# Running the 64-row matmuls of a four-sublayer streaming-encoder trunk over 128 rows, with zeros in the unwanted rows

## The chip, the cores and the metric

One core of one Trainium2 chip runs the whole program; the other cores are idle. The metric is the time of one execution on the device in microseconds (us), median over the runs shown. Engines by the names of the profile: PE is TensorE's matmul, PEld its weight load, DVE is VectorE, ACT is ScalarE, POOL is GpSimd, SP is SyncE, which here only issues DMAs.

## The reference, cut to what matters

The input is 256 positions of 2048 features. Layer 0 mixes by a chunked gMLP and a Mamba-2 scan side by side, layer 1 by multi-head latent attention; each is followed by a gated MLP with a causal convolution, and a final RMS norm ends it. Everything is fp32. The two places that the change touches are these lines of the reference:

```python
# Mamba-2: decay between positions, from the cumulated a = dt * A of each of 32 heads
a_cum = jnp.cumsum(da, -1)
decay = jnp.exp(segsum(da))                 # exp(a_cum[i] - a_cum[j]), lower triangle
y_diag = jnp.einsum("bcgls,bcgels,bcsgep->bclgep", cb, decay, xd)
...
# attention: 16 heads; the scores are a sum of a 128-wide part and a rotary part of 64
sc = (jnp.einsum("bqhd,bkhd->bhqk", q_nope[:, q0:kend], k_nope[:, :kend])
      + jnp.einsum("bqhr,bkr->bhqk", q_pe[:, q0:kend], k_pe[:, :kend]))
```

The rotary key `k_pe` is one for all heads; the rotary query is one of 64 rows for each head.

## The kernel before, in words

**Weights.** All weights stream once from memory in units of 128 x 1024 fp32 (`load`, L167), and each unit is turned into a pair of float32r parts, `hi` by an ACT copy (L198) and `lo` by a DVE subtraction (L199). `AHEAD, LOADS = 2, 3` (L162) says how many units ahead of the matmuls a unit is converted and loaded. Activations are kept as the same kind of pair side by side in one 128 x 512 tile.

**Matmul loops.** `wstat` (L237) holds a 128 x 128 weight tile still and streams the activations: one matmul of 512 columns with `hi`, one of 256 with `lo`, for each weight tile. `astat` (L250) holds the activations and streams the weights: three matmuls of 416 or 512 columns for each half of the positions. Both write the PSUM tiles `acc`. Between them, `tick()` runs one step of a background generator from the list `bg`, so that smaller work is woven into the long matmul loops at places fixed in the code; a scheduler then sets each engine's order from the program's dependences.

**Layer 0, the scan.** `dt_prep` (L498) leaves the cumulated decays of 32 heads in `cst` (L469), a tile of 64 partitions: rows 0 to 31 hold the float32r high part of each head's sums over 256 positions, rows 32 to 63 the low part (L533, L534). `selr` is a constant that picks rows h and h + 32. `ssd(g)` (L612), a background generator run once for each of four groups of eight heads, does four steps of two heads. Each step broadcasts the two heads' sums to all 128 partitions by two matmuls over 64 rows (L627), lets DVE (L634), ACT (L636) and DVE (L641) make the decay matrices from them, and multiplies these with the inputs by matmuls of 64 columns, 128 rows deep (L652). There are 32 broadcasts in all.

**Layer 1, attention.** `latent_out` (L841) makes the rotary key: its 64 columns of weights are given twice, so that rows 0 to 63 and 64 to 127 of `kr` are equal. `roped` (L830) rotates them and writes `krope` (L814), 128 rows by 256 positions. The loop at L933 handles two heads per turn: six `wstat` calls of four weight tiles each make the rotary queries of both heads (64 rows each in one 128-row tile `qr`), two queries and two keys. The scores of the heads before (`scores`, L876), the transposes of their probabilities (`turn`, L896) and the products with the values (`values`, L902) stand between these calls. For each head and each half of the queries, `scores` issues a matmul over 128 rows and then one over 64 rows into the same columns of PSUM, all four in plain fp32, which the profile records as two matmuls each:

```python
r0 = (hh % 2) * 64
for t, (o, n) in enumerate(HALF):           # n = 128, then 256 columns
    mm(ps[:, o:o + n], qn[:, t * P:(t + 1) * P], kk[:, :n], start=True, stop=False)
    mm(ps[:, o:o + n], qr[r0:r0 + 64, t * P:(t + 1) * P], krope[r0:r0 + 64, :n], start=False, stop=True)
```

**Buffers.** 2 KB tiles come from `slot()` (61 buffers), 1 KB tiles from `tmp()` (10 buffers), PSUM from two pools of four banks, `acc` and `ms`.

Of the kernel before, what the change touches and what calls it, by code (L numbers as in the profile page):

```python
# [17 lines left out]
P = 128  # L18
# [16 lines left out]

# [1 line left out]
def stat_stream(w, cols=None, front=0):  # L37
    """[K, N] -> units [U, 128, 1024]: eight 128x128 tiles each, k fastest;
    of the first `front` column tiles the last two k tiles come after the rest."""
    if cols is not None:  # L40
        w = w[:, cols]
    k, n = w.shape
    t = w.reshape(k // P, P, n // P, P).transpose(2, 0, 1, 3)
    if front:
        a = t[:front]
        t = np.concatenate([a[:, :-2].reshape(-1, P, P), a[:, -2:].reshape(-1, P, P), t[front:].reshape(-1, P, P)])
    t = t.reshape(-1, 8, P, P)
    return np.ascontiguousarray(t.transpose(0, 2, 1, 3)).reshape(-1, P, 1024)


def mov_stream(w, cw):
    """[K, N] -> units [U, 128, 2*cw]: two k tiles of a chunk of cw columns each."""
    k, n = w.shape
    t = w.reshape(k // 256, 2, P, n // cw, cw).transpose(3, 0, 2, 1, 4)
    return np.ascontiguousarray(t).reshape(-1, P, 2 * cw)
# [43 lines left out]

# [1 line left out]
@with_exitstack  # L101
def trunk(ctx: ExitStack, tc: tile.TileContext, a, out):
# [40 lines left out]

# [1 line left out]
    seq = []  # L145
# [21 lines left out]
    def load():  # L167
        """one DMA of weights; the first ones bring the input along."""
        i = st["load"]
        if i >= len(seq):  # L170
            return
        st["load"] += 1
        ap, u, wd = seq[i]
        raw = wp.tile([P, 1024], F32, tag="raw", name=nm("raw"), bufs=4)[:, :wd]
        nc.sync.dma_start(out=raw, in_=ap[u])
        raws.append(raw)
        if i == 0:
            nc.sync.dma_start(out=vec[:, :KD], in_=a["vec"][:, :KD])
        if i < KD // 2:
            nc.sync.dma_start(out=h2[i], in_=a["x0"][i])  # L180
        if i == KD // 2:
            nc.sync.dma_start(out=con, in_=a["con"])
            nc.sync.dma_start(out=vec[:, KD:], in_=a["vec"][:, KD:])

    def convert():
        """weights as a pair of float32r parts whose sum is exact."""
        i = st["conv"]
        if i >= len(seq):
            return
        st["conv"] += 1  # L190
        raw, wd = raws[i], seq[i][2]
        raws[i] = None
        hi = wp.tile([P, 1024], F32R, tag="hi", name=nm("hi"))
        lo = wp.tile([P, 1024], F32R, tag="lo", name=nm("lo"))
        n = 2 if i < 2 else 1
        for c in range(n):
            q = slice(c * wd // n, (c + 1) * wd // n)
            A.copy(out=hi[:, q], in_=raw[:, q])  # L198
            V.tensor_tensor(lo[:, q], raw[:, q], hi[:, q].bitcast(F32), op=ALU.subtract)  # L199
        ready.append((hi, lo))  # L200
# [20 lines left out]

# [1 line left out]
    bg = []  # L223
# [47 lines left out]
    def split(src, scale=None, dst=None):  # L271
        """[128,256] fp32 (SBUF or PSUM), times a per-partition scale -> [hi | lo]."""
        x = slot(F32R) if dst is None else dst
        if scale is None:
            A.copy(out=x[:, :S], in_=src)
            V.tensor_tensor(x[:, S:], src, x[:, :S].bitcast(F32), op=ALU.subtract)  # L276
        else:
            A.activation(x[:, :S], src, AF.Identity, bias=0.0, scale=scale)  # L278
            V.scalar_tensor_tensor(x[:, S:], src, scale, x[:, :S].bitcast(F32), op0=ALU.mult, op1=ALU.subtract)  # L279
        return x  # L280

    def newton(y, v, t):
        """y = v ** -0.5"""
        V.tensor_scalar(y.bitcast(I32), v.bitcast(I32), -0.5, 1597463007.0, op0=ALU.mult, op1=ALU.add)
        for _ in range(3):
            V.tensor_tensor(t, y, y, op=ALU.mult)
            V.scalar_tensor_tensor(t, t, -0.5, v, op0=ALU.mult, op1=ALU.mult)
            V.scalar_tensor_tensor(y, t, 1.5, y, op0=ALU.add, op1=ALU.mult)
# [6 lines left out]

# [1 line left out]
    warm = cp.tile([P, 512], mybir.dt.bfloat16, name="warm")  # L297
# [5 lines left out]

# [1 line left out]
    con = cp.tile([P, CONST.shape[1]], F32, name="con")  # L305
# [13 lines left out]

# [1 line left out]
    class Sq:  # L321
        """sum of squares over feature tiles; the last tile goes its own way."""

# [45 lines left out]
        def spread(self, n):  # L369
            """the factor for feature-major tiles alone, on every partition."""  # L370
            ps = pmis()
# [8 lines left out]
    def pending(sq, n=D, wait=6, hold=None):  # L380
        """the RMS factor, made a few steps into the next matmuls."""
        box = {}

        def gen():
            for _ in range(wait):
                yield
            box["v"] = sq.finish(n, hold) if hold else sq.spread(n)
            yield

        bg.append(gen())  # L390
        return box

# [1 line left out]
    class Lazy(list):  # L394
        """entries are made when the matmul loop first reaches them."""

# [16 lines left out]

    # small tables that the layers read later
    row = cp.tile([P, 96], F32, name="row")
# [5 lines left out]
    def small_loads():  # L421
        pin(nc.gpsimd.dma_start(out=row, in_=a["row"].partition_broadcast(P)))
        yield
        for i in range(2):
            # spatial weights [j, g, i], block-lower-triangular part
            pin(nc.gpsimd.dma_start(out=wsT[i], in_=a["wsT"][:, i * 512:(i + 1) * 512]))
# [10 lines left out]

# [1 line left out]
    cosT = cp.tile([P, S], F32, name="cosT")  # L439
# [23 lines left out]

    # ================= layer 0 mixer =================
    dtt = cp.tile([P, 2, 32], F32, name="dtt")
    cum = cp.tile([P, 2, 32], F32, name="cum")
    w0 = cp.tile([P, 32], F32, name="w0")
    e1 = cp.tile([P, 32], F32, name="e1")
    cst = cp.tile([64, S], F32R, name="cst")  # L469

    def gate_z(pst, c):
        """silu of a chunk of z; for chunk 0 the first 32 columns are dt."""
        o = []
# [24 lines left out]
    def dt_prep():  # L498
# [15 lines left out]
        for t in range(2):  # L514
            for r in range(2):
                V.scalar_tensor_tensor(dad[:, t, r, :], dtt[:, t, :], -1.0, ea, op0=ALU.mult, op1=ALU.mult)
        pin(V.tensor_copy(out=selr, in_=C("sel")))
        for _ in range(20):
            yield
# [11 lines left out]
        for t in range(2):  # L531
            mm(ps[:64, t * P:(t + 1) * P], dad[:, t].rearrange("p a b -> p (a b)"), C("tri"), start=True, stop=True)
        A.copy(out=cst, in_=ps[:64, :S])  # L533
        V.tensor_tensor(cst[32:64, :], ps[32:64, :S], cst[32:64, :].bitcast(F32), op=ALU.subtract)  # L534
# [5 lines left out]
    def conv_tile(b, wname, n, width, taps, bias):  # L540
        """causal depthwise conv of a [128,256] tile along the free axis."""
        o = tmp()
# [69 lines left out]
    def ssd(g):  # L612
# [10 lines left out]
        for hp in range(4):  # L623
            ps = pmis()
            for i in range(2):
                hh = h0 + 2 * hp + i
                mm(ps[:, i * S:(i + 1) * S], selr[:64, hh:hh + 1].to_broadcast([64, P]), cst, start=True, stop=True)  # L627
            yield
# [34 lines left out]

    # gMLP, four chunks of 512 channels, the scan's groups woven in
    ya, late = [], []
# [48 lines left out]

    # gating by z, grouped RMS norm, back to feature-major
    yb = [None] * 16
# [35 lines left out]
    def residual(kt, xin, wname, last=False, front=0):  # L752
        """front: that many tiles run ahead through all but the last two k tiles."""
        sq = Sq()
# [54 lines left out]

    # ================= layer 1 mixer (MLA) =================  # L810
    box = pending(sq)
    ckv, cq, sk, sqq = [], [], Sq(), Sq()
    kr = slot()[:, :S]
    krope = slot()[:, :S]  # L814

# [14 lines left out]
    def roped(x, o):  # L830
        """rotate the halves of two 64-row heads."""
        G.tensor_tensor(o, x, cosT, op=ALU.mult)
# [8 lines left out]
    def latent_out(i, ps):  # L841
        if i == 4:
            scaled(ps, kr)
            roped(kr, krope)
            return
# [30 lines left out]
    def scores(hh, qr, qn, kk):  # L876
        ps = pmis()
        r0 = (hh % 2) * 64
        for t, (o, n) in enumerate(HALF):
            mm(ps[:, o:o + n], qn[:, t * P:(t + 1) * P], kk[:, :n], start=True, stop=False)  # L880
            mm(ps[:, o:o + n], qr[r0:r0 + 64, t * P:(t + 1) * P], krope[r0:r0 + 64, :n], start=False, stop=True)
        sc = slot()
# [29 lines left out]
    def step(kind, j):  # L912
        """one stage of the attention of heads 2j and 2j + 1."""
        if not 0 <= j < 8:
# [53 lines left out]

# [1 line left out]
    _, R, Rp = sq.finish(D)  # L970
# [84 lines left out]
```

## Time and profile before

| what | value |
|---|---|
| median of 3 runs | 2423.49 us |
| the three runs | 2418.5, 2423.49, 2424.66 us |
| the profiled execution: span from first to last instruction (its time is not listed apart from the runs) | 2419.3 us |
| PE busy | 2386.0 us, 99% of the span, 13479 matmul records |
| PEld busy | 2072.6 us, 86% |
| DVE, ACT, POOL busy | 1582.7 us (65%), 1189.3 us (49%), 482.7 us (20%) |
| mean granted TensorE clock | 0.995 of full speed |
| DMA | 0.6 of the engines' time, 180 GB/s |

Matmuls are pipelined: a record of one matmul overlaps the next one's, so a busy share of 99% does not by itself say that the array is fed without pause. The spacing of the starts says that, and the timeline gives the starts. The timeline merges instructions of the same line, operation and tiles into one row, and shows the form (rows * columns of the weights, then the streamed shape) of the first of them.

### The profile page before, as it was taken

How to read it: one execution, taken by the hardware profiler on the slowest of the kernel's cores; microseconds unless marked ns; L12 is line 12 of the kernel's file. 1: busy time of each engine (PE TensorE's matmuls, PEld its weight loads, DVE VectorE, ACT ScalarE, POOL GpSimd, SP SyncE). 2: the span in 40 equal slices, each digit the busy share in tenths (PEclk: the TensorE clock that was granted, in tenths of full speed). 3: DMA queues.
4: the chain of work that ended last, by engine and by line, in shares of the span. 5: the costliest groups of instructions: out<-in, count | busy, mean ns of one | idle time of the engine just before them, and what ended most of it. 6: DMA issues, size and time to landing. Idle time of an engine off the chain costs nothing.

```text
span 2419.3 us, 35301 instructions
## 1 busy us (share of the span) xinstructions
PE 2386.0 (99%) x13479; PEld 2072.6 (86%) x13479; DVE 1582.7 (65%) x2371; ACT 1189.3 (49%) x1729; POOL 482.7 (20%) x452
## 2 busy tenths in 40 slices
PE   8999999999999999999999999999999999999997
PEld 6888888988888888888888887788888888888886
DVE  7677777665576666666555577778666666664544
ACT  5654444644455555555444445544555555554442
POOL 4111221022211112111111132123211111111111
PEclk9999999999999999999999999999999999999998
DMA  6565545666666666666666655356666666666664
GB/s 219 166 178 156 160 153 153 188 184 189 184 190 188 189 191 191 191 189 189 191 190 191 190 170 155 96 158 185 196 188 189 190 191 191 188 190 190 191 191 131
DMA packets 121913, 435.54 MB, mean 180 GB/s; under 512 B 13696, under 2 KB 14080, under 8 KB 121744
## 3 DMA queue, kind: packets, MB, share of 16 engines
q1 hardware_dynamic: 120672, 431.02, 59.3%
q8 instruction: 105, 1.72, 0.3%
q0 software_dynamic: 352, 1.10, 0.2%
q10 hardware_dynamic: 720, 1.18, 0.1%
q14 instruction: 64, 0.52, 0.1%
HBM read 431.15 MB, written 2.10 MB: 179 GB/s over the span
## 4 chain that ended last, share of the span: by engine, by line
PE 95%; DVE 2%; issue 1%; POOL 1%; ACT 1%; DMA 0%; SPq 0%; DVEq 0%; POOLq 0%; ACTq 0%
PE acc L133 91%; PE ms L133 4%; DVE lo L199 1%; PE ms L136 1%; DVE s L279 0%; ACT hi L198 0%; DMA raw<-in_z 0%; POOL t L550 0%; DVE t L545 0%; DVE s L979 0%; POOL s L818 0%; DVE s L276 0%; POOL t L331 0%; DVE s L634 0%; DVE t L268 0%
## 5 line engine op out<-in xcount | busy, mean ns | idle before, releaser
L133 PE MATMUL acc<-s,hi 128*128 128x512 f32 x5936 | 2072.9, 394 | 0.0
L133 PE MATMUL acc<-s,lo 128*128 128x256 f32 x5936 | 1656.4, 279 | 3.8 <-DVE lo L199 3.8
L199 DVE TENSOR_TENSOR lo<-raw,hi 128x1024 fp32r<-128x1024 f32 (+2 forms) x824 | 1015.9, 1233 | 700.1 <-ACT hi L198 693.9
L198 ACT CAST hi<-raw 128x1024 fp32r<-128x1024 f32 (+2 forms) x824 | 858.0, 1042 | 1088.3 <-PE acc L133 883.4
L133 PEld LDWEIGHTS acc<-s,hi 128*128 128x128 f32 x5936 | 1112.4, 187 | 255.6 <-issue 3.2
L133 PEld LDWEIGHTS acc<-s,lo 128*128 128x128 f32 x5936 | 1118.8, 188 | 5.6 <-DVE lo L199 4.8
L133 PE MATMUL acc<-hi,s 128*128 128x512 f32 (+1 forms) x640 | 198.6, 385 | 6.2 <-DVE s L279 5.7
L331 POOL TENSOR_TENSOR t<-h 128x256 f32<-128x256 f32 x60 | 66.9, 1114 | 588.1 <-DVE h L771 563.9
L801 POOL TENSOR_TENSOR t<-t,R 128x256 f32<-128x256 f32 x88 | 121.4, 1380 | 313.8 <-ACT t L800 309.9
L798 POOL TENSOR_TENSOR t<-t,R 128x256 f32<-128x256 f32 x88 | 68.9, 783 | 488.7 <-DVE t L268 453.4
L133 PEld LDWEIGHTS acc<-hi,s 128*128 128x128 f32 x640 | 121.4, 192 | 23.7 <-DVE s L279 8.4
L545 DVE SCALAR_TENSOR_TENSOR t<-t,vec,t 128x255 f32<-128x255 f32 (+2 forms) x248 | 120.7, 487 | 14.2 <-ACT t L543 9.7
L133 PE MATMUL acc<-lo,s 128*128 128x416 f32 (+1 forms) x320 | 121.8, 381 | 1.4 <-DVE lo L199 1.4
L268 DVE TENSOR_TENSOR t<-acc,t 128x256 f32<-128x256 f32 x233 | 97.4, 418 | 0.8 <-ACT t L267 0.8
L267 ACT COPY t<-acc 128x256 f32<-128x256 f32 x233 | 83.5, 359 | 0.3 <-PE acc L133 0.3
L133 PE MATMUL ms<-s,s 128*128 128x128 f32 (+4 forms) x424 | 78.2, 307 | 1.1 <-DVE s L930 0.6
L133 PEld LDWEIGHTS ms<-s,s 128*128 128x128 f32 (+1 forms) x424 | 60.1, 189 | 19.9 <-issue 9.0
L342 POOL TENSOR_TENSOR sqacc<-sqacc,t 128x256 f32<-128x256 f32 x60 | 72.8, 1213 | 4.7
L543 ACT ACTIVATE t<-t,vec 128x256 f32<-128x256 f32 x112 | 67.2, 600 | 12.9 <-POOL t L798 7.6
L133 PEld LDWEIGHTS acc<-lo,s 128*128 128x128 f32 x320 | 61.5, 192 | 8.4 <-DVE lo L199 2.1
L279 DVE SCALAR_TENSOR_TENSOR s<-h,vec,s 128x256 fp32r<-128x256 f32 x64 | 56.6, 895 | 1.0 <-ACT s L278 1.0
L803 DVE TENSOR_TENSOR t<-t,t 128x256 f32<-128x256 f32 x88 | 37.4, 426 | 28.6 <-POOL t L801 28.6
(174 smaller groups left out, 811.7 us busy)
## 6 DMA issues: line engine op xcount, KB each, us to landing
raw<-in_up SPq DMA_DIRECT2D x352, 512.0 KB, 4.2
raw<-in_down SPq DMA_DIRECT2D x176, 512.0 KB, 3.6
raw<-in_wout SPq DMA_DIRECT2D x64, 512.0 KB, 3.6
raw<-in_z SPq DMA_DIRECT2D x40, 416.0 KB, 3.6
raw<-in_x SPq DMA_DIRECT2D x32, 512.0 KB, 3.6
raw<-in_v SPq DMA_DIRECT2D x32, 512.0 KB, 3.7
raw<-in_u SPq DMA_DIRECT2D x32, 512.0 KB, 3.9
raw<-in_wo SPq DMA_DIRECT2D x32, 512.0 KB, 3.6
```

The costliest lines, as they stand in the source:

```text
L133: return nc.tensor.matmul(*args, **kw)
L198: A.copy(out=hi[:, q], in_=raw[:, q])
L199: V.tensor_tensor(lo[:, q], raw[:, q], hi[:, q].bitcast(F32), op=ALU.subtract)
L267: A.copy(out=b, in_=ps[:, S:])
L268: V.tensor_tensor(b, ps[:, :S], b, op=ALU.add)
L279: V.scalar_tensor_tensor(x[:, S:], src, scale, x[:, :S].bitcast(F32), op0=ALU.mult, op1=ALU.subtract)
L331: eng.tensor_tensor(q, src, src, op=ALU.mult)
L342: eng.tensor_tensor(self.acc, self.acc, q, op=ALU.add)
L543: A.activation(o, b, AF.Identity, bias=bias, scale=taps[width - 1])
L545: V.scalar_tensor_tensor(o[:, i:], b[:, :S - i], taps[width - 1 - i], o[:, i:], op0=ALU.mult, op1=ALU.add)
L798: G.tensor_tensor(b, b, R, op=ALU.mult)
L801: G.tensor_tensor(o, o, R, op=ALU.mult)
```

## The change

The matmuls over 64 rows become matmuls over 128 rows. In the scan, `cst` has 128 partitions; rows 64 to 127 are set to zero once by a DVE multiplication of a constant with 0, and the broadcast uses all 128 rows of `selr` and `cst`. In attention, `krope` becomes 512 wide: columns 0 to 255 hold the rotated key in rows 0 to 63 and zeros below, columns 256 to 511 hold zeros and the key in rows 64 to 127. Two POOL memsets write the zeros; `roped` writes a 1 KB tile `ro`, and two ACT copies of 64 rows move it into place. `scores` streams 128 rows of `krope`, from the half that belongs to the head, against all 128 rows of `qr`. (The change also drops comments and docstrings.)

```diff
-    cst = cp.tile([64, S], F32R, name="cst")
+    cst = cp.tile([P, S], F32R, name="cst")
...
         pin(V.tensor_copy(out=selr, in_=C("sel")))
+
+        pin(V.tensor_scalar(cst[64:], con[64:, :S], 0.0, None, op0=ALU.mult))
...
-        A.copy(out=cst, in_=ps[:64, :S])
+        A.copy(out=cst[:64], in_=ps[:64, :S])
...
-                mm(ps[:, i * S:(i + 1) * S], selr[:64, hh:hh + 1].to_broadcast([64, P]), cst, start=True, stop=True)
+                mm(ps[:, i * S:(i + 1) * S], selr[:, hh:hh + 1].to_broadcast([P, P]), cst, start=True, stop=True)
...
-    krope = slot()[:, :S]
+
+    krope = slot()
+    G.memset(krope[64:, :S], 0.0)
+    G.memset(krope[:64, S:], 0.0)
...
             scaled(ps, kr)
-            roped(kr, krope)
+            ro = tmp()
+            roped(kr, ro)
+            for e in range(2):
+                A.copy(out=krope[e * 64:(e + 1) * 64, e * S:(e + 1) * S], in_=ro[e * 64:(e + 1) * 64])
             return
...
-        r0 = (hh % 2) * 64
+        r0 = (hh % 2) * S
         for t, (o, n) in enumerate(HALF):
             mm(ps[:, o:o + n], qn[:, t * P:(t + 1) * P], kk[:, :n], start=True, stop=False)
-            mm(ps[:, o:o + n], qr[r0:r0 + 64, t * P:(t + 1) * P], krope[r0:r0 + 64, :n], start=False, stop=True)
+            mm(ps[:, o:o + n], qr[:, t * P:(t + 1) * P], krope[:, r0:r0 + n], start=False, stop=True)
```

The order of PE is the same in both kernels, matmul for matmul. On PE, in the scan of the second group, the order after the change reads as follows (`ms` <- `s`,`s` are the products of 64 columns, `cst`,`selr` the broadcasts, `acc` the long loop):

```order
L133 MATMUL ms_2412<-s_1449,s_2395 128x64
L133 MATMUL ms_2426<-cst,selr 128x256
L133 MATMUL ms_2411<-s_1434,s_2395 128x64
L133 MATMUL ms_2426<-cst,selr 128x256
L133 MATMUL ms_2412<-s_1449,s_2395 128x64
L133 MATMUL ms_2461<-cst,selr 128x256 x2
L133 MATMUL acc_2373<-hi_2419,s_231 128x512
```

Nothing moved there: each group has two broadcasts that stand alone between products and three pairs.

On ACT, where the latents of layer 1 are made, the order before (`hi` is a converted weight unit, `s`<-`s`,`vec` the normed key latents):

```order
L278 ACTIVATE s_13422<-s_13265,vec 128x256
L267 COPY t_13460<-acc_13326 128x256
L198 CAST hi_13493<-raw_13469 128x1024
L278 ACTIVATE s_13430<-s_13318,vec 128x256
L267 COPY t_13514<-acc_13402 128x256
L198 CAST hi_13524<-raw_13491 128x1024
```

and after the change:

```order
L278 ACTIVATE s_13428<-s_13268,vec 128x256
L267 COPY t_13466<-acc_13329 128x256
L198 CAST hi_13499<-raw_13475 128x1024
L852 COPY s_13052<-t_13398 64x256 x2
L278 ACTIVATE s_13436<-s_13321,vec 128x256
L267 COPY t_13520<-acc_13408 128x256
L198 CAST hi_13530<-raw_13497 128x1024
```

The two copies into `krope` stand between a weight conversion and the last normed latent.

On POOL, at the start of the same stage, the order after the change:

```order
L342 TENSOR_TENSOR sqacc_11102<-sqacc_11102,t_12921 128x256
L818 MEMSET s_13052 64x256
L819 MEMSET s_13052 64x256
L823 TENSOR_TENSOR s_13161<-t_13162,R_13098 128x256
```

The two memsets stand between the last sum of squares of the layer before and the first scaled latent. Beside these, DVE has the one multiplication into `cst` (after the cast of `selr`, L517), and ACT's copy into `cst` (L533) now stands one place earlier, ahead of a silu.

## Rows read from the trace of the kernel before

**Rows 1.** The page: the span, PE's busy time, and the chain of work that ended last by engine and line.

```profile
span 2419.3 us, 35301 instructions
PE 2386.0 (99%) x13479; PEld 2072.6 (86%) x13479; DVE 1582.7 (65%) x2371; ACT 1189.3 (49%) x1729; POOL 482.7 (20%) x452
...
PE 95%; DVE 2%; issue 1%; POOL 1%; ACT 1%; DMA 0%; SPq 0%; DVEq 0%; POOLq 0%; ACTq 0%
```

**Rows 2.** Groups of instructions by line and shape, whole span: the matmuls over 64 rows on PE, weight loads over 128 and 64 rows on PEld (columns: rows * columns of the weights, streamed shape, count | busy us, mean ns | idle before, us), and ACT's weight conversion with what it waited for.

```profile
L133 PE MATMUL ms<-s,s 64*128 64x256 f32 x32 | 11.1, 428 | 0.0
L133 PE MATMUL ms<-cst,selr 64*128 64x256 f32 x32 | 9.0, 341 | 0.0
L133 PE MATMUL ms<-s,s 64*128 64x128 f32 x32 | 7.8, 322 | 0.0
...
L133 PEld LDWEIGHTS ms<-s,s 128*128 128x128 f32 x360 | 50.7, 190 | 12.7 <-issue 3.7 <-DVE s L930 0.9 <-DVE s L641 0.7
L133 PEld LDWEIGHTS ms<-s,s 64*128 64x128 f32 x64 | 9.4, 184 | 7.2 <-issue 5.3
...
L198 ACT CAST hi<-raw 128x1024 fp32r<-128x1024 f32 x782 | 822.4, 1052 | 1054.9 <-PE acc L133 859.8 <-issue 191.3 <-DVE lnt L286 1.8
```

**Rows 3.** Timeline of PE in the scan (columns: start us, us, engine, line, operation, tiles, form of the first, count).

```profile
297.35 0.60 PE L133 MATMUL ms<-s,s 128*128 128x128 f32 x4
...
298.02 0.39 PE L133 MATMUL acc<-lo,s 128*128 128x512 f32 x1
298.24 0.40 PE L133 MATMUL acc<-hi,s 128*128 128x512 f32 x1
298.57 0.50 PE L133 MATMUL ms<-cst,selr 64*128 64x256 f32 x2
...
299.34 0.40 PE L133 MATMUL acc<-lo,s 128*128 128x512 f32 x1
```

**Rows 4.** Timeline of PE at a sum of squares: two records of 256 columns in fp32 over 128 rows, in the long loop.

```profile
1675.57 0.59 PE L133 MATMUL ms<-sqacc,con 128*128 128x256 f32 x2
...
1676.24 0.28 PE L133 MATMUL acc<-s,lo 128*128 128x256 f32 x1
1676.36 0.39 PE L133 MATMUL acc<-s,hi 128*128 128x512 f32 x1
```

**Rows 5.** Timeline of PE at the scores of two heads, from their first matmul to the second matmul of the loop that follows.

```profile
1509.68 4.14 PE L133 MATMUL ms<-s,s 128*128 128x128 f32 x16
1513.75 0.50 PE L133 MATMUL acc<-s,hi 128*128 128x512 f32 x1
1514.09 0.28 PE L133 MATMUL acc<-s,lo 128*128 128x256 f32 x1
```

**Rows 6.** Timeline of PEld, the weight loads, at the first head of the same scores, up to the second head's first load (in brackets: idle time before, and what ended it).

```profile
1509.57 1.14 PEld L133 LDWEIGHTS ms<-s,s 128*128 128x128 f32 x6
1511.04 0.29 PEld L133 LDWEIGHTS ms<-s,s 64*128 64x128 f32 x2 [0.33 <-issue]
1511.66 1.13 PEld L133 LDWEIGHTS ms<-s,s 128*128 128x128 f32 x6 [0.33 <-issue]
```

**Rows 7.** Timeline of PE in the scan's second group: the broadcasts that stand alone, and (from 262.46) products of 64 columns with no broadcast between.

```profile
254.39 0.67 PE L133 MATMUL ms<-s,s 128*128 128x64 f32 x4
254.99 0.38 PE L133 MATMUL ms<-cst,selr 64*128 64x256 f32 x1
...
255.66 0.38 PE L133 MATMUL ms<-cst,selr 64*128 64x256 f32 x1
...
256.34 0.50 PE L133 MATMUL ms<-cst,selr 64*128 64x256 f32 x2
...
262.46 0.55 PE L133 MATMUL ms<-s,s 128*128 128x64 f32 x4
...
263.13 0.55 PE L133 MATMUL ms<-s,s 128*128 128x64 f32 x4
```

**Rows 8.** Timelines of ACT and DVE ahead of the product at 254.39, and of DVE at the first softmax.

```profile
250.47 1.06 ACT L198 CAST hi<-raw 128x1024 fp32r<-128x1024 f32 x1 [1.36 <-PE acc L133]
253.91 1.12 DVE L641 SCALAR_TENSOR_TENSOR s<-s,dtt,s 128x128 f32<-128x128 f32 x4
1488.68 0.56 DVE L883 TENSOR_TENSOR s<-ms,con 128x384 f32<-128x384 f32 x1 [1.53 <-PE ms L133]
```

**Rows 9.** Busy time of each engine in one turn of the attention loop (columns: window, length, busy us and count of PE, PEld, DVE, ACT, POOL, granted clock, DMA share, GB/s).

```profile
1513.20:1526.40 13.20, 13.20 (x75) 10.48 (x75) 10.72 (x29) 6.76 (x19) 3.43 (x6) 1.00 0.37 115
```

**Rows 10.** The rows nearest to the added instructions, by line and shape (a POOL memset, a DVE multiplication with a constant, ACT's copy into `cst`), and ACT's and POOL's timelines where the latents are made.

```profile
L427 POOL MEMSET s<- 64x256 f32 x2 | 0.8, 382 | 10.9 <-DMA s<-in_wsT 10.9
L452 DVE TENSOR_SCALAR t<-t 128x256 f32<-128x256 f32 x1 | 0.3, 293 | 0.0
L533 ACT CAST cst<-ms 64x256 fp32r<-64x256 f32 x1 | 0.4, 366 | 0.5 <-PE ms L133 0.5
1444.07 0.51 ACT L278 ACTIVATE s<-s,vec 128x256 fp32r<-128x256 f32 x1 [1.00 <-DVE s L826]
1410.10 1.70 POOL L818 TENSOR_TENSOR s<-t,R 128x256 f32<-128x256 f32 x1 [23.71 <-DVE R L288]
```

**Rows 11.** Busy time and granted clock in two stretches of the scan's third group (columns as in rows 9).

```profile
307.00:310.40 3.40, 3.19 (x17) 2.22 (x15) 3.40 (x9) 1.18 (x2) 0.00 (x0) 1.00 0.51 159
310.50:314.00 3.50, 3.50 (x9) 2.77 (x9) 1.47 (x6) 0.10 (x1) 0.00 (x0) 0.51 0.61 164
```

## The prediction

> **What bounds the kernel now.** I read the page first. PE is busy for 2386.0 of 2419.3 us and carries 95% of the chain that ended last [rows 1], so a PE microsecond saved is a microsecond of the result wherever no other engine is close behind. The second view says whether one is: ACT's weight conversion sat idle for 1054.9 us in all, 859.8 of them until PE was through with a buffer [rows 2]. The converters wait for PE, not PE for them. What is left to ask is what the array does inside its 99%, and that needs the timelines, where the distance from one start to the next is the price of a matmul.
>
> The prices over 128 rows come from undisturbed places. Four fp32 records of 128 columns and one float32r matmul of 512 take 298.02 − 297.35 = 0.67 us, and the 512 columns alone 298.24 − 298.02 = 0.22 [rows 3]; with 0.23 for it, a record of 128 columns is 0.11. Two records of 256 columns and the 512 take 1676.24 − 1675.57 = 0.67, so such a record is 0.22; the float32r matmul of 256 columns is 1676.36 − 1676.24 = 0.12 [rows 4].
>
> Now the same sums where rows change. The scores of two heads are 16 fp32 records, eight of 128 and eight of 256 columns, alternating between 128 and 64 rows. With one 512 behind them they should take 8 x 0.11 + 8 x 0.22 + 0.23 = 2.87 us. They take 1514.09 − 1509.68 = 4.41 [rows 5]. The weight loads show where it goes: at the changes between 128 and 64 rows that come behind 256 columns, the load begins late, after 0.33 us of idle time that ends by "issue", no other engine [rows 6] (behind 128 columns the gap is too short to split the row). The reader should see that the next load doesn't run under the matmul before, as it does elsewhere. And the first matmul after the last change takes 1514.09 − 1513.75 = 0.34 instead of 0.23 [rows 5].
>
> **What the change removes.** Scores: 4.41 − 2.87 = 1.54 us for two heads, eight times: **12.3 us**. Broadcasts: a pair between two matmuls of 512 columns takes 299.34 − 298.24 = 1.10 us, against 2 x 0.23 + 2 x 0.12 = 0.70 [rows 3, 4]: 0.40. Three pairs in each of four groups make 12 x 0.40 = 4.8 us. The two that stand alone: eight records of 64 columns and two broadcasts take 256.34 − 254.39 = 1.95 us. Four such records and a 512 take 263.13 − 262.46 = 0.67, so 0.11 each, and the whole should take 8 x 0.11 + 2 x 0.12 = 1.12 [rows 4, 7]. Of the 0.83 between them some 0.09 is the way into the pair that follows, counted with the pair; 0.74 x 4 = 3.0 us, of which I take 2.8, since the first of those records were also waiting on DVE's last product there [rows 8]. Broadcasts in all: **7.6 us**. Sum: 19.9 us. The rows changed are 64 + 32 records [rows 2]; each 64-row run of a score has two changes, 64 in all, and five runs of broadcasts in each of four groups have 40, so 104 changes at 0.19 us.
>
> Does a change cost nothing once both sides have 128 rows? The matmul streams the same columns and gets as many weight columns, and the 128-row records around it show no gap when `ms` follows `acc` or fp32 follows float32r [rows 3, 4]. The bounds of what goes: from nothing to all 19.9. I take all, since the rows over 128 rows are the very same instructions but for the rows.
>
> [...]
>
> **What it adds.** One DVE multiplication of 64 x 256, by the nearest row 0.29 us [rows 10], behind the sums that PE waits for in that place, once: nothing, and 0.3 us if it were all on the path. Two POOL memsets of 0.38 us each, at a place where POOL then sits idle for 23.71 us [rows 10]: nothing as long as their buffer is free, and with all of it on the path 0.8. Two ACT copies of 64 x 256, 0.37 us each by the copy into `cst`; they stand ahead of a latent for which ACT idles for 1.00 us [rows 10], so 0.74 fits, and 0.7 is the bound from above. ACT's copy into `cst`, one place earlier, adds nothing: it is the same work. No DMA is added or moved.
>
> **What could be late next.** A faster PE arrives earlier at work that DVE and ACT prepare. In the scan, the first product at 254.39 [rows 7] follows closely on DVE's four matrices, begun at 253.91 and all done at 255.03; the chain in front of them begins with a weight conversion that waited 1.36 us for PE to free its buffer [rows 8]. So it starts earlier when PE is earlier, and the small slack stays what it is. At the first softmax DVE waited 1.53 us for PE's scores [rows 8], so that chain moves along too. In a turn of the attention loop DVE is busy for 10.72 us of 13.20 [rows 9]; the turn shrinks to 13.20 − 1.54 = 11.7, still above 10.72. I put 0 to 2 us on all of this and take 0.4.
>
> **The sum.** 19.9 − 0.4 = 19.5 us off the profiled execution's span of 2419.3. That span lies 4.2 us under the median of the runs shown, 2423.5, and close to their fastest; I set the difference against the median: 2423.5 − 19.5 = **2404.0 us**.
>
> **The rivals.**
>
> *Waits take the gain back (0.08).* If DVE is the true pace of the scan, the products wait for what the broadcasts saved and all 7.6 us there are lost; and if DVE's turn, 10.72 us with no idle time allowed, stretches by one late conversion of some 1.2 us, the eight turns lose most of (11.7 − 10.72), say 0.6 each, 4.8 us. For it: DVE is the second busiest engine, with the slacks above. Against: the converters' waits on PE [rows 2, 8]. Time: 2423.5 − 19.9 + 7.6 + 4.8 = 2416.
>
> *Rows don't matter (0.05).* The pause might belong to the fp32 rotary operands or to the accumulation into the same columns, not to the 64 rows; then it stays, and the time stays at 2423.5. Against: fp32 over 128 rows runs without it [rows 4], and the broadcasts, which are float32r and don't accumulate, have it too [rows 3]. [...] The loads themselves agree (184 ns over 64 rows, 190 over 128 [rows 2]); it is the wait in front of them that is lost.
>
> *The clock falls (0.03), slower.* [...]
>
> **How the numbers follow.** The forecast has 0.84. Its own range: from 2404.0 down by 1.7 for the clock and 3 for the scatter of the runs, up by 3.4 (all added work and waits at their bounds, 3.8, less the 0.4 taken) and 3: 2399 to 2410. To leave out no more than 2 in 10, I keep that and widen it by one to two microseconds, for prices that I read from one place each: 2398 to 2412. A change within 0.3% (7.3 us), about what a measurement here can tell from none, lies between 2416.2 and 2430.8. The first rival's 2416 is at that border; half of it counts as faster. Faster: 0.84 + 0.04 = 0.88. Same: 0.05 + 0.04 = 0.09. Slower: 0.03.
>
> **What would show it.** On the timeline of PE, the scores of two heads with the 512 behind should take 2.9 us, not 4.41, in all eight turns, and a pair of broadcasts with its neighbours 0.70, not 1.10. The weight loads of these should show no idle time by "issue". If these spacings shrink and the end doesn't move, new idle time must stand on PE, ended by DVE's matrices of the scan or its softmax, and the first rival is right. If the spacings stay with all rows at 128, my reading of the pause is wrong. A granted clock below 0.99 in many of the scan's stretches would speak for the third.

## The result and the profile after

The changed kernel takes 2402.03 us, median of 4 runs (2400.11 to 2403.32); the kernel before takes 2421.69, median of 4 (2418.5 to 2424.66). The ratio is 0.9925 with an interval of 0.9912 to 0.9938, so it is faster by 18.2 us (15.0 to 21.3); the medians differ by 19.7. The forecast was 2404.0 with a range of 2398 to 2412. The profiled execution is the one of 2403.32 us, with a span of 2401.5.

The page of the changed kernel, the same lines as [rows 1]: the span, the busy times, and the chain that ended last.

```profile
span 2401.5 us, 35306 instructions
PE 2368.9 (99%) x13479; PEld 2078.8 (87%) x13479; DVE 1584.1 (66%) x2372; ACT 1189.9 (50%) x1731; POOL 482.5 (20%) x454
...
PE 95%; DVE 3%; issue 1%; ACT 1%; POOL 1%; DMA 0%; SPq 0%; DVEq 0%; POOLq 0%; ACTq 0%
```

PE has the same 13479 records and 17.1 us less busy time; the span fell by 17.8. The chain is still PE's. DVE's share of it reads 3% instead of 2%; the view rounds to whole per cent, so that step says little by itself. Where DVE came in is shown below.

The matmuls that were widened, grouped by line and shape as in [rows 2] (columns: rows * columns of the weights, streamed shape, count | busy us, mean ns | idle before).

```profile
L133 PE MATMUL ms<-s,s 128*128 128x64 f32 x128 | 19.1, 259 | 1.6 <-DVE s L643 1.6
L133 PE MATMUL ms<-s,s 128*128 128x256 f32 x64 | 16.5, 380 | 0.0
...
L133 PE MATMUL ms<-cst,selr 128*128 128x256 f32 x32 | 7.9, 313 | 0.0
```

No group with 64 rows is left. The 256-column records of the scores took 11.2 us for 32 and 11.1 for another 32 before; all 64 now take 16.5. The first row shows something new: 1.6 us of idle time in front of the scan's products, ended by DVE's decay matrices.

The timeline of PE at the scores of two heads, the same matmuls as in [rows 5].

```profile
1501.54 2.86 PE L133 MATMUL ms<-s,s 128*128 128x128 f32 x16
1504.05 0.58 PE L133 MATMUL acc<-s,hi 128*128 128x512 f32 x1
1504.47 0.28 PE L133 MATMUL acc<-s,lo 128*128 128x256 f32 x1
```

1504.47 − 1501.54 = 2.93 us, against 4.41 before and 2.87 forecast. Of the eight turns six take 2.85; this one and the first, with 2.96, are the longest. The weight loads of the same stretch, as in [rows 6]:

```profile
1501.51 2.49 PEld L133 LDWEIGHTS ms<-s,s 128*128 128x128 f32 x16
```

One unbroken row where there were three with gaps of 0.33 us. A pair of broadcasts between long matmuls, as in [rows 3], here in the scan's second group:

```profile
244.93 0.40 PE L133 MATMUL acc<-hi,s 128*128 128x512 f32 x1
245.16 0.40 PE L133 MATMUL ms<-cst,selr 128*128 128x256 f32 x2
...
245.65 0.39 PE L133 MATMUL acc<-lo,s 128*128 128x512 f32 x1
```

From the start ahead of the pair to the second one behind it: 245.65 − 244.93 = 0.72, against 1.10 before and 0.70 forecast.

Where did the 17.8 us of the span come from? PE's order is the same in both kernels, so the starts of the same matmul can be subtracted, place by place. The scores in the eight turns of attention are shorter by 1.48 to 1.57 us each, 12.4 us together. The first group of the scan is shorter by 1.29, the second by 1.31, the fourth by 1.36, and the third by 2.95, of which some 1.6 is a clock fall that is gone. That makes 19.3. Two new clock falls take 1.6 and 1.45 of it back, and 1.14 of the second is regained where PE waited before (further down). The remaining 0.4 us is spread.

### The profile page after: what moved, and what is told of

Read it like the earlier page. It is cut to its first block, busy times and chain, and to the rows that moved or that the text cites. A ratio compares the mean times of both kernels' runs of the same rounds, so it can differ in the third digit from the quotient of the medians.

```text
span 2401.5 us, 35306 instructions
## 1 busy us (share of the span) xinstructions
PE 2368.9 (99%) x13479; PEld 2078.8 (87%) x13479; DVE 1584.1 (66%) x2372; ACT 1189.9 (50%) x1731; POOL 482.5 (20%) x454
## 4 chain that ended last, share of the span: by engine, by line
PE 95%; DVE 3%; issue 1%; ACT 1%; POOL 1%; DMA 0%; SPq 0%; DVEq 0%; POOLq 0%; ACTq 0%
PE acc L133 91%; PE ms L133 3%; DVE lo L199 1%; PE ms L136 1%; ACT hi L198 0%; DVE s L279 0%; POOL t L552 0%; DMA raw<-in_z 0%; DVE t L547 0%; DVE s L987 0%; DVE s L276 0%; POOL t L683 0%; DVE s L636 0%; DVE t L268 0%; POOL t L841 0%
## 5 line engine op out<-in xcount | busy, mean ns | idle before, releaser
L198 ACT CAST hi<-raw 128x1024 fp32r<-128x1024 f32 (+2 forms) x824 | 858.4, 1042 | 1079.2 <-PE acc L133 875.6
L268 DVE TENSOR_TENSOR t<-acc,t 128x256 f32<-128x256 f32 x233 | 97.0, 416 | 0.8 <-ACT t L267 0.8
L133 PE MATMUL ms<-s,s 128*128 128x128 f32 (+3 forms) x424 | 66.6, 292 | 2.2 <-DVE s L643 1.6
L133 PEld LDWEIGHTS ms<-s,s 128*128 128x128 f32 x424 | 59.9, 190 | 9.7 <-issue 3.5
```

The source lines that it names most:

```text
L133: return nc.tensor.matmul(*args, **kw)
L268: V.tensor_tensor(b, ps[:, :S], b, op=ALU.add)
```

## The experiments

The kernel before ran beside each of them. Its median was 2420.17 (19 runs) beside the two with one part alone, the reordered scores and the two halves of the rows, 2420.38 (17 runs) beside the dummies and the added work, and 2420.19 (9 runs) beside the two with a multiplication moved to DVE.

**Each part alone.** The theory was that the change is a sum of two savings on PE with one price per change of rows, so that attention alone gives the 12.3 us that the prediction's sum has for it. The first kernel is the changed one with the scan put back:

```diff
-    cst = cp.tile([P, S], F32R, name="cst")
+    cst = cp.tile([64, S], F32R, name="cst")
...
-        pin(V.tensor_scalar(cst[64:], con[64:, :S], 0.0, None, op0=ALU.mult))
...
-                mm(ps[...], selr[:, hh:hh + 1].to_broadcast([P, P]), cst, start=True, stop=True)
+                mm(ps[...], selr[:64, hh:hh + 1].to_broadcast([64, P]), cst, start=True, stop=True)
```

> The attention half of the change alone: scores over 128 rows, the scan's broadcasts still over 64. [...] Rival (waits on DVE take the gain back in attention): under 8 us off, and new idle time on PE by the softmax.

Measured: 2406.94 us, ratio 0.9944 (0.9932 to 0.9957), 13.2 us faster. In its trace the scores of two heads take 2.85 us in six of eight turns, and 2.92 in the turn shown above.

The second is the changed kernel with attention put back:

```diff
-    krope = slot()
-    G.memset(krope[64:, :S], 0.0)
-    G.memset(krope[:64, S:], 0.0)
+    krope = slot()[:, :S]
...
-            mm(..., qr[:, t * P:(t + 1) * P], krope[:, r0:r0 + n], start=False, stop=True)
+            mm(..., qr[r0:r0 + 64, t * P:(t + 1) * P], krope[r0:r0 + 64, :n], start=False, stop=True)
```

> The scan's half of the change alone: broadcasts over 128 rows, scores as before. Theory with the full price: 40 changes go, 7.6 us off. What the trace after shows instead: 1.3 to 1.4 us off in each of the later three groups, so 5.4 us off, because the first product of a group then waits for DVE for about 0.5 us where it waited for 0.2 or less. Rival (rows don't matter): 0.

Measured: 2414.25 us, ratio 0.9977 (0.9967 to 0.9986), 5.9 us faster. The two parts add up to 19.1 us, the whole of the change (18.2 by the ratio, 19.7 by the medians). Attention gave what the sum had for it, the scan less, though the interval (3.4 to 8.0 us) alone does not exclude the 7.6 of the forecast; the matched starts of the changed kernel, 1.3 us for a group instead of 1.9, do.

**Is it the change of rows, or the 64-row matmul itself?** Both would have given the same forecast. The third kernel is the one before, with all its matmuls over 64 rows, in another order: the scores of a head run over 128, 64, 64, 128 rows. That leaves 32 of the 64 changes in the scores.

```diff
         for t, (o, n) in enumerate(HALF):
-            mm(..., qn[...], kk[...], start=True, stop=False)
-            mm(..., qr[r0:r0 + 64, ...], krope[r0:r0 + 64, ...], start=False, stop=True)
+            for r in ((0, 1) if t == 0 else (1, 0)):   # r = 1: the rotary part
+                mm(..., start=(r == t), stop=(r != t))
```

> The kernel before, with 64-row matmuls everywhere, but the scores of a head issued as 128, 64, 64, 128 rows instead of 128, 64, 128, 64: two changes a head instead of four, the same matmuls. Theory (a price for each change): 32 changes go, 32 x 0.195 = 6.2 us off. Rival (a price for each 64-row matmul, or for the fp32 rotary operands): 0.

Measured: 2415.22 us, ratio 0.9976 (0.9967 to 0.9985), 5.0 us faster. The timeline of PE at the scores of two heads in this kernel:

```profile
1507.04 3.56 PE L133 MATMUL ms<-s,s 128*128 128x128 f32 x16
...
1510.67 0.28 PE L133 MATMUL acc<-s,lo 128*128 128x256 f32 x1
```

3.63 us, as in all eight turns but the first, half way between 4.41 and the 2.85 of most turns after the change: half of the changes, half of the price, with every 64-row matmul still there. So the price belongs to the change. 0.78 x 8 = 6.2 us for 32 changes is 0.195 each.

**The price of one change by itself.** Three kernels each add 88 small float32r matmuls of 128 columns to the changed kernel, one at a time inside the long loops of the gated MLPs, between matmuls over 128 rows (their results are used nowhere):

```diff
             psg = wstat(KD, xs)
+            mm(dps[:, :P], cst[:64, :P], cst[:64, P:], start=True, stop=True)   # 64 rows
+            mm(dps[:, :P], cst[:, :P], cst[:, P:], start=True, stop=True)       # or: 128 rows
+            mm(dps[:64, :P], cst[:, :64], cst[:, P:], start=True, stop=True)    # or: 64 columns
             psv = wstat(KD, xs)
```

> The changed kernel with one more matmul, of no use to the result, in each of the 88 steps of the two gated MLPs, between two long loops: float32r, 128 columns, over 64 rows. Theory: each costs its own 0.05 to 0.11 us and two changes of rows, 2 x 0.19 us: 38 to 43 us more than the changed kernel. Rival (a price for each 64-row matmul, not for the change back): half of that.

> The same 88 added matmuls over 128 rows. Theory: 0.05 to 0.11 us each, 5 to 10 us more than the changed kernel, so 33 us less than with 64 rows.

> The same 88 added matmuls over 128 rows but with 64 columns of weights, so that they write 64 partitions. If a change in the columns of the array costs what a change in its rows does: 38 to 43 us more than the changed kernel. If it costs nothing: 5 to 10.

Measured, one execution each: spans of 2468.2, 2432.0 and 2438.1 us. What costs is the difference between the kernels: (2468.2 − 2432.0) / 88 = 0.41 us for a lone matmul over 64 rows, 0.206 for each of its two changes. By matched starts 36.1 of these 36.2 us stand in the loops with the dummies. PE's timeline at one dummy over 64 rows:

```profile
721.82 0.28 PE L133 MATMUL acc<-s,lo 128*128 128x256 f32 x1
722.03 0.32 PE L133 MATMUL ms<-cst 64*128 64x128 f32 x1
722.29 0.50 PE L133 MATMUL acc<-s,hi 128*128 128x512 f32 x1
722.62 0.28 PE L133 MATMUL acc<-s,lo 128*128 128x256 f32 x1
```

and over 128 rows:

```profile
720.69 0.28 PE L133 MATMUL acc<-s,lo 128*128 128x256 f32 x1
720.80 0.22 PE L133 MATMUL ms<-cst 128*128 128x128 f32 x1
720.86 0.45 PE L133 MATMUL acc<-s,hi 128*128 128x512 f32 x1
721.15 0.28 PE L133 MATMUL acc<-s,lo 128*128 128x256 f32 x1
```

From the first start to the last, 0.80 against 0.46 us. The start before the dummy is 0.21 away instead of 0.11, the dummy itself holds the array for 0.26 instead of 0.06, and the one behind it for 0.33 instead of 0.29. The loss stands in front of both changes and a little behind. It is 0.34 us at the dummy, 0.17 for a change, on the average of all 88 too; the other 0.07 is spread over the matmuls between the dummies, and what causes it was not found. The waits of the weight loads (PEld, us in total, times, longest) show it in the kernel with 64 rows,

```profile
PEld ms L133 <- issue: 26.9, 97, 1.0
```

and in the one with 128 rows:

```profile
PEld ms L133 <- issue: 4.7, 9, 1.0
```

88 more waits, 22 us more: idle time of the weight load "by issue" is the sign by which such a change is recognised in these profiles. In the kernel before the same line had 12.6 us in 36 waits, in the changed one 4.8 in 9.

Over 64 columns the span is 6.1 us longer than over 128. Between single executions that is not clear of scatter: the kernel before ran from 2415.44 to 2424.69. At the dummies nothing is lost: from the start ahead to the second one behind it is 0.46 us on average, the same as with 128 columns, and the waits "by issue" are 4.5 us in 9. The 5.0 us by which the loops are longer by matched starts are spread over the other matmuls. So a price of a change of columns does not show here.

The size of the dummies was not as expected: even those over 128 rows, which hold the array for 0.06 us, made the span 30.5 us longer than the changed kernel's. That is taken up in the last section.

**The added work alone.** The changed kernel with its memsets, copies, multiplication and buffers, and all its matmuls put back to 64 rows:

```diff
-                mm(ps[...], selr[:, hh:hh + 1].to_broadcast([P, P]), cst, start=True, stop=True)
+                mm(ps[...], selr[:64, hh:hh + 1].to_broadcast([64, P]), cst[:64], start=True, stop=True)
...
+        r1 = (hh % 2) * 64
...
-            mm(..., qr[:, t * P:(t + 1) * P], krope[:, r0:r0 + n], start=False, stop=True)
+            mm(..., qr[r1:r1 + 64, t * P:(t + 1) * P], krope[r1:r1 + 64, r0:r0 + n], start=False, stop=True)
```

> All that the change adds (the memsets, the multiplication into the decay tile, the two copies into the wider key tile), but every matmul over 64 rows as before. Theory (the added work lies beside other work): no change from before within 1 us, and the spacings of PE as before. Rival (the added work is on the path): up to 1.8 us more. If the gain came from the new layout and not from the rows, it would show here: 18 us off.

Measured: 2421.48 us, ratio 1.0006 (0.9997 to 1.0016). The added work costs nothing that shows, and the layout without the rows wins nothing.

**Where the scan's missing gain went.** In the changed kernel PE waits at the first product of a group. These are the waits of its PE for the scan's products (us in total, times, longest):

```profile
PE ms L133 <- DVE s L643: 1.6, 3, 0.6
```

Before it was 0.4 us in 2 waits. PE's timeline at the one in the second group, the place of [rows 7] (in brackets: idle time before, and what ended it):

```profile
254.71 0.67 PE L133 MATMUL ms<-s,s 128*128 128x64 f32 x4 [0.50 <-DVE s L643]
...
255.87 0.49 PE L133 MATMUL ms<-cst,selr 128*128 128x256 f32 x2
```

From 254.71 to the second pair's start at 255.87 it is 1.16 us, against 1.95 before: the broadcasts that stand alone gave all that was forecast. What is lost stands in front. The chain of work that leads to this product in the changed kernel, followed back from each step to what released it (start us, us, what; pauses left out):

```profile
246.32 0.43 DVE t L268
...
246.82 0.79 POOL t L683
...
247.63 0.04 ACT t L684
...
247.95 1.05 ACT hi L198
...
249.02 0.36 DVE lo L199
...
250.87 1.26 DVE s L276
252.14 1.04 DVE s L636 x4
253.17 0.74 DVE lo L199
...
254.23 0.35 DVE s L643
```

Before, this product's chain ran over PE alone. In the third group, where PE already waited 0.2 us before, it entered the same steps in another place:

```profile
299.07 2.28 PE acc L133 x9
...
301.38 1.06 ACT hi L198
...
302.46 0.34 DVE lo L199
```

Both chains meet at ACT's weight conversion (`hi` L198). On ACT it stands behind the gelu L684 (the gMLP's activation, woven between the scan's steps), and it also needs a buffer that PE frees. Before, PE's buffer came last; after, the gelu does, and its branch (L268, POOL L683, ACT L684) goes back to ACT's conversion at 244.10, ahead of the first pair at 245.16. From the meeting point on DVE runs in its own order: conversion, L276, L636, conversion, L643.

The distances say the same. In the changed kernel the long matmul ahead of the first pair starts at 244.93, DVE's L268 at 246.32, the product at 254.71: 1.39 and 8.39 us. In the kernel before the product starts at 254.39 [rows 7] and the other two here:

```profile
244.62 0.40 PE L133 MATMUL acc<-hi,s 128*128 128x512 f32 x1
246.01 0.42 DVE L268 TENSOR_TENSOR t<-acc,t 128x256 f32<-128x256 f32 x1
```

1.39 and 8.38. Between a point ahead of the pair and the product nothing became shorter, although PE has 0.38 less to do there; that 0.38 is what the wait took. ACT's conversion did come a little earlier, 1.63 us behind L268 instead of 1.74, but DVE's conversion behind it took 1.93 us instead of 1.79. The conversion that the prediction looked at, at 250.47 before, did move with PE: 4.46 us behind L268 before, 4.08 after. But it is not in this chain. The exponential behind it now waits for DVE at its end, and is done before L643 starts:

```profile
253.21 0.63 ACT L638 ACTIVATE s<-s 128x512 f32<-128x512 f32 x1 [0.45 <-DVE s L636]
```

A further kernel tried to shorten the gelu branch: the multiplication of L683 goes from POOL (0.78 us, and a way there) to DVE.

```diff
-        G.tensor_tensor(b, b, R, op=ALU.mult)
+        V.tensor_tensor(b, b, R, op=ALU.mult)
```

> The changed kernel with one multiplication of the gating moved from POOL to DVE (16 times). Theory on the scan's missing 2 us: the first product of a group waits for a chain that starts before the first broadcast pair, by way of POOL's multiplication, ACT's gelu and weight conversion and DVE; 0.4 us less in that chain makes the three waits of 0.5 us on DVE's matrices fall to 0.1 or so, some 1.2 us off the changed kernel (less than the runs scatter; the idle time on PE decides). Rival (the chain starts at PE's freeing of a weight buffer, as the prediction had it): the waits stay at 0.5 us.

Measured: 2400.48 us, ratio 0.9920 (0.9908 to 0.9933). The number that it was made for, PE's waits for the products:

```profile
PE ms L133 <- DVE s L643: 2.2, 3, 0.7
```

They grew from 1.6 to 2.2 us: as a remedy it failed. The timeline says why. Here the long matmul ahead of the first pair starts at 241.72, and these are DVE's L268, DVE's conversion and the product:

```profile
243.63 0.42 DVE L268 TENSOR_TENSOR t<-acc,t 128x256 f32<-128x256 f32 x1
...
246.06 1.93 DVE L199 TENSOR_TENSOR lo<-raw,hi 128x1024 fp32r<-128x1024 f32 x1 [1.42 <-ACT hi L198]
...
251.75 0.67 PE L133 MATMUL ms<-s,s 128*128 128x64 f32 x4 [0.74 <-DVE s L643]
```

From L268 on the chain is indeed shorter, 8.12 us instead of 8.39, and all of it in front of DVE's conversion: 2.43 us instead of 2.70; behind it, 5.69 in both. But L268 itself starts 1.91 us behind the long matmul instead of 1.39: 0.52 lost, 0.27 won. DVE was held up ahead of it at 241.54, where it waited 1.06 us for the same branch one step earlier, whose POOL operation L685 took 1.46 us there and 0.74 in the changed kernel. So the product follows the gelu branch in both directions, as this theory has it; that the branch can be shortened with a gain was not shown. The median is 1.6 us under the changed kernel's, within the intervals, and these waits do not explain it.

**Using both halves of the rows.** If the change of rows is the price, there is another way to avoid it: run the 64-row matmuls of both heads next to each other, over rows 0 to 63 and 64 to 127. The kernel has the scan of the changed one; the scores of two heads go 128, 64, 64, 128 with the heads alternating inside, so two changes are left for each two heads, 16 in all. (`a` and `b` are the operands, for the rotary part rows 64 e to 64 e + 63.)

```diff
+    def score_mms(qr, q, k):
+        pss = [pmis(), pmis()]
+        for t, (o, n) in enumerate(HALF):
+            for r in ((0, 1) if t == 0 else (1, 0)):    # r = 1: the rotary part
+                for e in range(2):
...
+                    pin(mm(pss[e][:, o:o + n], a, b, start=(r == t), stop=(r != t)))
```

> The scan over 128 rows as after the change; the scores over 64 rows, but with the 64-row matmuls of two heads (rows 0 to 63 and 64 to 127) next to each other, in the order of first half, second half, and one run of them for two heads: two changes in each turn instead of eight. Theory (a price for each change, and 64-row matmuls one after the other): 5.4 off by the scan and 48 x 0.195 = 9.4 by the scores, 14.8 off, 3 us slower than the changed kernel. If matmuls on different rows of the array run at the same time, their eight records (2.6 us of a turn after the change: 1.3 on 64 rows) take half, 0.65 us less a turn, 5 us: then 20 off, 2 us faster than the changed kernel. Rival (a price for each 64-row matmul): 5.4 off.

Measured: 2398.63 us, ratio 0.9911 (0.9897 to 0.9924), 21.5 us faster than before. PE's timeline at the scores of two heads:

```profile
1499.41 2.52 PE L133 MATMUL ms<-s,s 128*128 128x128 f32 x16
...
1502.00 0.28 PE L133 MATMUL acc<-s,lo 128*128 128x256 f32 x1
```

2.59 us with two changes left in it, where the changed kernel has 2.93 in this turn and 2.85 in six of eight. The groups of 64-row matmuls in this kernel:

```profile
L133 PE MATMUL ms<-s,s 64*128 64x256 f32 x32 | 4.8, 377 | 0.0
...
L133 PE MATMUL ms<-s,s 64*128 64x128 f32 x32 | 3.9, 322 | 0.0
```

One still lasts 377 or 322 ns, yet the busy time fell from 11.1 to 4.8 and from 7.8 to 3.9 us [rows 2]: two of them run at once. Over the whole of attention less is left of this. Between two matmuls with the same place in PE's order, one ahead of the first scores and one behind the last (at 1477.49 and 1594.34 us before), there are 116.85 us before, 104.21 in the changed kernel and 103.27 here: 0.94 us won on the changed kernel. What takes the rest was not traced. The median is 3.4 us lower, but the granted clock is 0.995 in this trace and 0.993 in the changed kernel's, where two clock falls cost 1.9 us (below), and the two ratios overlap, so the order of the medians is not certain.

The last kernel puts this together with the multiplication on DVE; its edit is the two above.

> The version with the 64-row matmuls of two heads side by side, and the gating's multiplication on DVE: 2 us off the changed kernel for the first (as measured before) and 1.2 for the second, 2397 to 2399 us where the kernel before has 2420 to 2422.

Measured: 2400.97 us, ratio 0.9918 (0.9905 to 0.9932): no better than the kernel before it.

## Why the prediction was right, step by step

**What bounds the kernel.** Right: PE's time went down by 17.1 us and the span by 17.8.

**The scores, 12.3 us.** Right in size and place: 12.4 by the matched starts, 13.2 with that part alone.

**The cause.** The prediction took the pause for a price of the change of rows, 0.19 us each. Reordered scores gave 0.195; the dummies gave 0.17 at the dummy itself and 0.206 with what is spread around it. The rival in which rows don't matter is refuted by each part alone and by the dummies. A rival that the prediction did not have, a price of each 64-row matmul whatever its neighbours, fits the result as well as its own reason did; only the reordered kernel tells them apart. Part of the price stands at the weight load that comes late: with the 88 dummies over 64 rows its waits "by issue" are 22 us longer, 0.25 us for each dummy, beside 0.41 us of span. What makes up the rest no run separates.

**The broadcasts, 7.6 us.** Mechanism right, size wrong: the scan gave 5.9 us alone, 5.2 to 5.4 by the matched starts (four groups at 1.29 to 1.36). Pairs and single ones are as short as forecast. The step that failed is "it starts earlier when PE is earlier, and the small slack stays what it is". It looked at ACT's conversion at 250.47, which follows PE but does not decide when the product can start. The conversion that does, one earlier, had two conditions of nearly equal time: PE's buffer and the gelu ahead of it on ACT. The gelu's branch goes back to a point ahead of the first pair and did not move. So the first pair's 0.38 became a wait, of 0.50 us in the second group. In the first group two waits for ACT's `t` take it, 0.29 us of the weight load at 189.97, right behind the pair, and PE's at 196.18, a matmul that starts at the same time in both kernels. Four pairs lose about 1.5 us of the 2.3 that are missing. Of the rest, some 0.2 for a group, half stands at the pair behind the single broadcasts: with these it gave 0.99 us by matched starts, where the sum has 0.70 + 0.40. The other pairs gave 0.38 instead of 0.40.

**What could be late next, 0.4 us taken.** Too little, by that 1.5 us, and inside the bound of 2 that was kept for the range. In attention no new wait came: DVE's 10.72 us did fit into the shorter turn. So the first rival, waits take the gain back, is true for a fifth of the scan's term, and not for the scores.

**Added work at nothing.** Right: 1.0006, 0.9997 to 1.0016.

**The clock.** The fall at 310.50 [rows 11] is gone, but others came. Busy times and granted clock in three stretches of the changed kernel (columns as in [rows 9]):

```profile
196.50:201.00 4.50, 4.50 (x16) 3.50 (x15) 3.50 (x9) 3.54 (x4) 0.00 (x0) 0.63 0.49 124
310.50:314.00 3.50, 3.50 (x20) 2.71 (x19) 2.74 (x11) 2.05 (x3) 0.00 (x0) 1.00 0.36 129
1438.50:1443.50 5.00, 3.25 (x10) 2.87 (x11) 5.00 (x7) 2.33 (x5) 4.00 (x4) 0.66 0.36 107
```

The second stretch ran 9 matmuls at 0.51 before and runs 20 at full clock now. The first and third have a mean between two levels, 1.00 and the 0.50 that stands in this trace from 1440.50 to 1442.00; each follows a wait of PE, of 1.88 us for ACT's `t` up to 196.18 and of 2.64 for DVE's conversion up to 1440.24. But the kernel before waits at the same two matmuls, 1.82 and 2.65 us, and keeps the full clock there (1.00 from 196.50 to 201.00, and from 1443.00 to 1448.00, around the second at 1445.56). And the mean granted clock of the kernel before goes from 0.991 to 0.995 in the 19 runs beside the two with one part alone, with nothing changed in it. So the falls come and go, and do not follow from what the change does to the scan. The third rival, a lower clock and a longer time, did not happen: the mean granted clock of the trace is 0.993, where it was 0.995 before. Matched starts put 1.6 and 1.45 us of loss at the two. Of the second, 1.14 us come back by 1470, most of it where PE waited 0.87 us for a norm's factor before and doesn't now. Net, 1.9 lost and 1.6 won back: the clock hardly moves the result. No run shows the 1.7 us that the forecast's range has for the clock; in its place matched starts show some 1.6 us for the fall that went, and the 1.6 and 1.45 for the two that came.

**The total.** The sum's 19.9 less the 2.3 that the scan missed is 17.6, beside 18.2 by the ratio and 19.7 by the medians; the forecast lies 2 us above the median. That this is so close is in part luck: 2423.5, from which it subtracts, was 3.3 us above 2420.17, the median of the 19 later runs of the kernel before, and a gain of 19.5 was 1.9 above 17.6; the two errors pull in opposite ways.

## What to carry to other kernels

In this stream of matmuls over 128 rows, a lone matmul over 64 rows costs 0.41 us more than one over 128. Look for idle time of the weight load that ends by "issue", count the changes, and pad to 128 rows with zeros, put the short ones next to each other, or, where there are two independent ones, run them on the two halves of the rows (2.93, 3.63 and 2.59 us here for the scores of two heads, which took 4.41). Padding was free here (a ratio of 1.0006 for the added work alone), where the zeros are written once and off the path. And before you let a slack "move along" with a faster engine, follow every chain into the waiting instruction back to where it starts, the engine's own order included: one that starts ahead of the saving doesn't move.

## What was not expected of the hardware

**The long loops slowed down around the dummies.** 88 matmuls of 0.06 us are 5.3 us, but the kernel with dummies over 128 rows is 30.5 us longer than the changed one. A stretch of 100 us in the last MLP, in the changed kernel (columns as in [rows 9]):

```profile
2100.00:2200.00 100.00, 100.00 (x579) 88.19 (x578) 56.47 (x69) 46.13 (x61) 15.79 (x15) 1.00 0.63 190
```

and with dummies over 128 rows:

```profile
2100.00:2200.00 100.00, 100.00 (x572) 87.16 (x571) 59.89 (x79) 48.79 (x71) 15.45 (x16) 1.00 0.60 187
```

Seven matmuls fewer at the same full clock. The slowing also stands in the down projections, where no dummy is: some 3.3 ns for each matmul, the same in all three kernels, so most of the 30.5 us cancels in the differences between them. There the starts no longer come in a steady step of 230 and 117 ns for the 512 and 256 columns of a weight tile, but go through 233 and 117, 241 and 120, 236 and 113 over and over. In a loop with dummies, too, three weight tiles take 1.06 us, from 911.86 to 912.92 with dummies over 128 rows, against 1.04 from 899.70 to 900.74 in the changed kernel. The cause was not found.

**DVE beside POOL.** POOL's operations of 512 columns in the scan's second group, and DVE's two weight conversions in the chain above:

```profile
249.82 3.22 POOL L622 TENSOR_TENSOR s<-s,row 128x512 f32<-128x512 f32 x2
```

```profile
249.02 1.93 DVE L199 TENSOR_TENSOR lo<-raw,hi 128x1024 fp32r<-128x1024 f32 x1 [2.02 <-ACT hi L198]
...
253.10 1.21 DVE L199 TENSOR_TENSOR lo<-raw,hi 128x1024 fp32r<-128x1024 f32 x1
```

While POOL runs, up to 253.04, DVE's conversion takes 1.93 us instead of 1.21, and L276 takes 1.26 at 250.87 where it took 0.42 at 244.20. This is part of why the branch over DVE is as long as it is. It was not varied.
